# Compression inputs of a sparse-attention trunk: scaled into SBUF in order of parity, moved between partitions by DMA, split once at 128x512

## Chip, core and metric

The kernel runs on one core of one Trainium2 chip. The metric is the time of one execution on the device in microseconds. Engines are named as in the profile: PE is TensorE (PEld its weight loads), DVE VectorE, ACT ScalarE, POOL GpSimd, SP the engine whose queue issues most DMAs.

## What is computed

One layer of a trunk with 256 tokens of width 1024: a sparse attention mixer (16 heads in 4 groups, head width 64), cross attention to 256 memory tokens, and a gated feed-forward layer with a short convolution. The change is in the compression of keys (input 0) and values (input 1) in the mixer. Each input is a 256-wide projection of the normalized tokens, 4 groups of 64. Blocks of 32 tokens at a stride of 16 (15 blocks a group) are flattened to 2048 numbers, a position code is added, and a two-layer network makes one key or value of each:

```python
def _compress(t, pe, w1, w2):
    B, S, G, dk = t.shape
    n_chunks = S // CMP_STRIDE
    r = CMP_BLOCK // CMP_STRIDE
    n_cmp = n_chunks - r + 1
    c = t.reshape(B, n_chunks, CMP_STRIDE, G, dk)
    blk = jnp.concatenate([c[:, j:j + n_cmp] for j in range(r)], axis=2)
    blk = (blk + pe[:, None, :]).transpose(0, 1, 3, 2, 4).reshape(B, n_cmp, G, CMP_BLOCK * dk)
    return jax.nn.gelu(blk @ w1) @ w2
```

## The kernel before

Everything is float32. A matmul operand is split in two parts for TensorE's rounded float32 format: hi, a copy rounded by ACT, and lo, the rest, by DVE (`split_hi`, L191; `split_lo`, L194). `mm3` (L184 to L189) then makes three matmuls of a product: hi x hi, lo x hi, hi x lo. Weights come as chunks of 128 x 2048, in halves of 128 x 1024: SP loads a half into a raw buffer (L112), ACT makes hi (L120), DVE makes lo (L124). Halves are split up to 4 ahead of the matmul that needs them (`half`, L127), and there are 6 buffers of hi and 6 of lo, taken in turn, so the hi of a half waits until the matmuls that read the half six places earlier are through.

The stage around the change is `first` (L667): the projection of input 0 (`compress_in(0)`, PSUM tile pc0), a quarter of the queries (pq0), the projection of input 1 (`compress_in(1)`, pc1), the selected keys (`keys(0)`, pk0), then `hidden(0)` and `hidden(1)`, then `keys(1)` and more queries. `hidden(j)` multiplies the compression's first-layer weights by the prepared input: 16 steps of two matmuls (hi and lo of the weights) into pM0 or pM1, whose stationary operand holds hi and lo of the input side by side. Its result is brought out by ACT (hsb), transposed (pH), and goes through the gelu on DVE and ACT.

The prepared input j is the pair of tiles c2[j][0] and c2[j][1] of 128 partitions x 8 steps x (hi, lo) x 64 columns. Two tokens that follow each other (even and odd, the parity) stand in the two halves of the partitions, and the two groups that a 128-partition projection holds must come side by side in the columns, so data move between the halves of the partitions. Before, `out` in `compress_in` (L459) scales pc in place by the row of reciprocal norms (L462), and then four `split_hi` and four `split_lo` (L475, L478), one for each pair of group half and parity, read 64 partitions of PSUM and write 64 other or equal partitions of SBUF. GpSimd then copies the columns shifted by one block into the second tile (L480) and puts the position code's part pe into the last column (L482). All of `hidden(j)` waits for these copies.

The order on SP and GpSimd is that of the program text (manual schedule). On PE, ACT and DVE a scheduler sets the order when the program is built, by an estimate of when each operation could run. On the chip each engine then works through its list in that order.

The PSUM tag S has two banks, which pc0, pc1, pk0, pM0, pM1 and pk1 take in turn. The scratch tile xT has 8 slices of 256; slice 0 holds the row of reciprocal norms.

## Time and profile before

| | |
|---|---|
| median of 3 runs | 458.88 us (458.44 to 459.89) |
| profiled execution | 459.02 us, span 457.1 us |
| PE busy | 445.2 us (97%) |
| DVE busy | 324.2 us (71%) |
| ACT busy | 288.9 us (63%) |
| POOL busy | 42.7 us (9%) |
| mean granted PE clock | 0.992 |

Times in the trace are us from the span's start; a row's second number is its duration, and a merged row (x4) gives the time of all. The profiled execution is 1.9 us longer than its span, which runs from the first to the last instruction. PE's ends are modelled: matmuls overlap, so the step from one start to the next is what one costs.

### The profile page before, as it was taken

Reading aid. Unit: us, or ns where it says so; the run is one execution under the profiler, and the core shown is the slowest. Engines: PE = TensorE matmul, PEld = TensorE weight load, DVE = VectorE, ACT = ScalarE, POOL = GpSimd, SP = SyncE. Lnnn points to the kernel's source line nnn. Section 1 sums busy time; section 2 is a strip of 40 time slices with the busy share of each in tenths; the row PEclk is TensorE's granted clock in tenths of the full one; section 3 lists DMA queues with packets and bytes.
Section 4 is the critical chain, followed back from the end, with each engine's and each line's share of the span. In section 5 each row is a group of like instructions: output and inputs, shape, how many; then the busy total and the mean of one; then the engine's idle time right before and its main releaser. Section 6 shows DMA issues by size and latency. Waiting matters only on the chain.

```text
span 457.1 us, 8682 instructions
## 1 busy us (share of the span) xinstructions
PE 445.2 (97%) x3276; PEld 412.1 (90%) x3276; DVE 324.2 (71%) x694; ACT 288.9 (63%) x591; POOL 42.7 (9%) x82
## 2 busy tenths in 40 slices
PE   8999799999999999999999999999999999999994
PEld 5999799999998778999998899999999999888984
DVE  4788989798888895846643857878777777745413
ACT  6796689677887886865553757666666666535301
POOL 4332001221200000200000010000000000001003
PEclk9999899999999999999999999999999999999998
DMA  8997775543422005555334437755555555564302
GB/s 293 363 412 261 242 241 167 181 122 111 139 94 92 3 1 181 162 156 187 102 104 170 150 128 210 246 186 184 187 180 185 184 189 179 189 188 151 128 0 93
DMA packets 22077, 77.05 MB, mean 169 GB/s; under 512 B 2579, under 2 KB 3091, under 8 KB 22035
## 3 DMA queue, kind: packets, MB, share of 16 engines
q1 hardware_dynamic: 21312, 74.39, 48.7%
q10 hardware_dynamic: 720, 2.10, 1.4%
q8 instruction: 26, 0.43, 0.4%
q14 instruction: 19, 0.13, 0.1%
HBM read 75.43 MB, written 1.05 MB: 167 GB/s over the span
## 4 chain that ended last, share of the span: by engine, by line
PE 85%; DVE 6%; DMA 4%; ACT 2%; issue 2%; SPq 0%; POOLq 0%; DVEq 0%; ACTq 0%; POOL 0%
PE up L187 8%; PE up L189 8%; PE up L188 8%; PE pd L189 5%; PE pd L187 4%; PE pd L188 4%; PE O L868 2%; DVE lo L124 2%; PE pt L846 2%; DMA raw<-in_w_ks 2%; PE pcq L187 2%; PE pmk L189 2%; PE pmk L188 2%; PE pmk L187 2%; PE pmv L189 2%
## 5 line engine op out<-in xcount | busy, mean ns | idle before, releaser
L124 DVE TENSOR_TENSOR lo<-raw,hi 128x1024 fp32r<-128x1024 f32 x130 | 158.6, 1227 | 60.2 <-ACT hi L120 59.3
L120 ACT ACTIVATE hi<-raw 128x1024 fp32r<-128x1024 f32 x130 | 136.8, 1058 | 55.1 <-PE pd L189 17.7
L187 PE MATMUL up<-h_hi,hi 128*128 128x256 f32 x304 | 86.3, 284 | 0.0
L189 PE MATMUL up<-h_hi,lo 128*128 128x256 f32 x304 | 86.2, 284 | 0.0
L188 PE MATMUL up<-h_lo,hi 128*128 128x256 f32 x304 | 86.2, 284 | 0.0
L188 PEld LDWEIGHTS up<-h_lo,hi 128*128 128x128 f32 x304 | 58.4, 192 | 0.0
L189 PEld LDWEIGHTS up<-h_hi,lo 128*128 128x128 f32 x304 | 58.4, 192 | 0.0
L187 PEld LDWEIGHTS up<-h_hi,hi 128*128 128x128 f32 x304 | 58.4, 192 | 0.0
L189 PE MATMUL pd<-hi,aT_lo 128*128 128x512 f32 (+1 forms) x110 | 38.5, 350 | 0.0
L188 PE MATMUL pd<-lo,aT_hi 128*128 128x512 f32 (+1 forms) x110 | 38.5, 350 | 0.0
L187 PE MATMUL pd<-hi,aT_hi 128*128 128x512 f32 (+1 forms) x110 | 38.4, 349 | 0.0
L832 ACT ACTIVATE pp<-pp,nm 128x128 f32<-128x128 f32 (+1 forms) x64 | 28.4, 447 | 5.8 <-DVE nm L826 5.6
L826 DVE CUSTOM_DVE_ANT_0 pp<-s,tri,nrs 128x128 f32<-128x128 f32 (+1 forms) x64 | 24.1, 412 | 2.4 <-PE pt L846 2.0
L188 PEld LDWEIGHTS pd<-lo,aT_hi 128*128 128x128 f32 x110 | 20.7, 188 | 2.9
L189 PEld LDWEIGHTS pd<-hi,aT_lo 128*128 128x128 f32 x110 | 20.7, 188 | 2.9
L187 PEld LDWEIGHTS pd<-hi,aT_hi 128*128 128x128 f32 x110 | 20.7, 189 | 2.9
L1110 ACT ACTIVATE th<-c 128x256 f32<-128x256 f32 x22 | 9.1, 414 | 22.2 <-DVE c L1108 22.2
L850 ACT ACTIVATE pT<-pt 128x256 f32<-128x256 f32 (+1 forms) x32 | 15.3, 482 | 9.2 <-PE pt L846 8.9
L840 DVE TENSOR_SCALAR pp<-pp,den 128x128 f32<-128x128 f32 (+1 forms) x64 | 19.8, 349 | 0.6
L189 PE MATMUL pmv<-hi,memT_lo 128*128 128x256 f32 x64 | 18.6, 290 | 0.0
L188 PE MATMUL pmv<-lo,memT_hi 128*128 128x256 f32 x64 | 18.5, 289 | 0.0
L189 PE MATMUL pq<-hT_hi,lo 128*128 128x256 f32 x64 | 18.5, 289 | 0.0
(309 smaller groups left out, 1149.2 us busy)
## 6 DMA issues: line engine op xcount, KB each, us to landing
raw<-in_w_up SPq DMA_DIRECT2D x44, 512.0 KB, 4.6
raw<-in_w_dn SPq DMA_DIRECT2D x20, 512.0 KB, 3.8
raw<-in_w_q SPq DMA_DIRECT2D x8, 512.0 KB, 5.1
raw<-in_w_mk SPq DMA_DIRECT2D x8, 512.0 KB, 5.0
raw<-in_w_mv SPq DMA_DIRECT2D x8, 512.0 KB, 3.7
raw<-in_w_out SPq DMA_DIRECT2D x8, 512.0 KB, 3.8
raw<-in_ca_wq SPq DMA_DIRECT2D x8, 512.0 KB, 4.7
raw<-in_ca_wo SPq DMA_DIRECT2D x8, 512.0 KB, 4.2
```

Of the source, the lines that this page charges most:

```text
L120: nc.scalar.activation(his[i][h], raws[i][h], AF.Copy)
L124: nc.vector.tensor_tensor(t, raws[i][h], f(his[i][h]), op=ALU.subtract)
L187: nc.tensor.matmul(ps, lh, rh, start=start, stop=False)
L188: nc.tensor.matmul(ps, lh, rl, start=False, stop=False)
L189: nc.tensor.matmul(ps, ll, rh, start=False, stop=stop)
L826: nc.vector.tensor_tensor_reduce(self.ppv[:, br], sv[:, br], tri[:, 1 - t:], nrs[:, t:t + 1], 3e38, ALU.add, ALU.min, self.nm[:, br:br + 1])
L832: nc.scalar.activation(self.ppv[:, br], self.ppv[:, br], AF.Exp, bias=self.nm[:, br:br + 1], scale=-1.0, accum_out=self.den[:, br:br + 1])
L840: nc.vector.tensor_scalar(self.ppv[:, br], self.ppv[:, br], den[:, br:br + 1], None, op0=ALU.mult)
L846: nc.tensor.transpose(self.pt[:, o:o + P], self.pp[:, o:o + P], ident)
L850: nc.scalar.activation(self.pT[:, :self.w], self.pt[:, :self.w], AF.Copy)
L868: nc.tensor.matmul(O[r:r + DK, m * P:(m + 1) * P], V[:, blk // 2, blk % 2, g, :], group[i].pT[:, blk * P:(blk + 1) * P], start=False, stop ...
L1110: nc.scalar.activation(th, c, AF.Tanh, scale=0.5)
```

## The change

`out` in `compress_in` now scales pc into one slice pair of xT, written in order of parity. Four DMAs on GpSimd's queue, one for each pair of group half and parity, move 64 partitions x 256 numbers each to a second slice pair, where parity stands in the halves of the partitions. After 6 further ticks of the schedule (CW) one `split_hi` and one `split_lo` of 128 x 512 write c2. Columns are now ordered by group first, 16 a group, with the position code's part at the 16th of the first group, so the hidden layer has 64 columns in place of 60 behind its matmuls. The two GpSimd copies by x (hi, lo) become one of 64 x 15 numbers a partition, and the two of pe become one. For input 0 the slices are 6, 7 and 2, 3; for input 1 they are 4, 5 and 6, 7; `keys(0)` and `keys(1)` scale into slices 2, 3 and 4, 5.

```diff
@@ compress_in @@
             NB = 15
-            NC = NB * G
+            NC = 64
+            PEC = NB
...
-                    both = ps.rearrange("p (m s) -> p m s", m=2)
-                    nc.vector.tensor_tensor(both, both, row.unsqueeze(1).to_broadcast([P, 2, S]), op=ALU.mult)
-                    split((B[1][:, :, 0, NC], B[1][:, :, 1, NC], cc[:, o + 8:o + 16]),
-                          (pe[:, 0, :, 0], pe[:, 1, :, 0], cc[:, o:o + 8]))
-                    yield
-                    items = []
+                    v, vp = (xT[:, k:k + 2].rearrange("p k s -> p (k s)") for k in ((6, 2), (4, 6))[j])
+                    v = v.rearrange("p (r m c) -> p r m c", r=2, m=2)
+                    vp = vp.rearrange("p (g c jj) -> p g c jj", g=2, jj=8)
+                    nc.vector.tensor_tensor(v.rearrange("p r m c -> p m c r"),
+                                            ps.rearrange("p (m c r) -> p m c r", m=2, r=2),
+                                            row.rearrange("p (c r) -> p c r", r=2).unsqueeze(1).to_broadcast(
+                                                [P, 2, 128, 2]), op=ALU.mult)
                     for gp in range(2):
                         for par in range(2):
-                            v_ = ps[gp * 64:gp * 64 + 64].rearrange(
-                                "p (m n jj r) -> p m n jj r", m=2, jj=8, r=2)[:, :, :, :, par]
-                            dh, dl = (B[0][par * 64:par * 64 + 64, :, x, :].rearrange(
-                                "p jj (n m gp) -> p m n jj gp", m=2, gp=2)[:, :, :, :, gp] for x in range(2))
-                            items.append((dh, dl, v_))
-                    for hi, lo, v_ in items:
-                        split_hi(hi, v_)
-                    yield
-                    for hi, lo, v_ in items:
-                        split_lo(lo, hi, v_)
-                    for x in range(2):
-                        nc.gpsimd.tensor_copy(B[1][:, :, x, 0:NC], f(B[0][:, :, x, G:16 * G]))
-                    for x in range(2):
-                        nc.gpsimd.tensor_copy(B[0][:, :, x, NC:NC + 1], f(pe[:, x]))
+                            nc.gpsimd.dma_start(vp[par * 64:par * 64 + 64, gp].rearrange("p c jj -> p (c jj)"),
+                                              v[gp * 64:gp * 64 + 64, par].rearrange("p m c -> p (m c)"))
+                    split((B[1][:, :, 0, 0, 0, PEC], B[1][:, :, 1, 0, 0, PEC], cc[:, o + 8:o + 16]),
+                          (pe[:, 0, :, 0], pe[:, 1, :, 0], cc[:, o:o + 8]))
+                    yield from pause(CW)
+                    hi, lo = (B[0][:, :, x].rearrange("p jj g m n -> p g (m n) jj") for x in range(2))
+                    split_hi(hi, vp)
+                    yield
+                    split_lo(lo, hi, vp)
+                    nc.gpsimd.tensor_copy(rows[1][:, :, 0:PEC], f(rows[0][:, :, 1:16]))
+                    nc.gpsimd.tensor_copy(B[0][:, :, :, 0, 0, PEC].rearrange("p jj x -> p x jj"), f(pe[:, :, :, 0]))
                     done.add(f"c2{j}")
```

The rest of the change follows the new order of the columns in `hidden`, `compressed_keys` and `compressed_values`.

The order in which the engines' lists stand moves at two places. In the names c200 and c201 are the two tiles of input 0, c210 and c211 those of input 1, and hi8_1 is the second half of weight chunk 8; chunk 5 is that of pk0, chunks 6 and 7 those of pM0, 8 and 9 those of pM1, 10 that of pk1.

The first place is ACT's list from the projections to the hidden layer. Before:

```order
L120 ACTIVATE hi5_0_363<-raw5_0_361 128x1024
L192 ACTIVATE c200_256<-pc0_260 64x2x16x8 x4
L120 ACTIVATE hi5_1_381<-raw5_1_379 128x1024
L611 ACTIVATE QS_240<-pq0_360 64x512 x2
L120 ACTIVATE hi6_0_456<-raw6_0_454 128x1024
L120 ACTIVATE hi6_1_478<-raw6_1_476 128x1024
L216 ACTIVATE sq_mem0a_1030,ss_mem0a_1029<-mem0_1001 128x512
L192 ACTIVATE c210_449<-pc1_453 64x2x16x8 x4
L894 DMA mem1_1052<-in_mem 128x1024
L120 ACTIVATE hi7_0_523<-raw7_0_521 128x1024
L585 ACTIVATE gsb_583<-pg_559 96x256
L120 ACTIVATE hi7_1_578<-raw7_1_576 128x1024
```

With the change:

```order
L121 ACTIVATE hi7_1_566<-raw7_1_564 128x1024
L193 ACTIVATE w2h_783<-w2k_245 128x256
L121 ACTIVATE hi8_0_627<-raw8_0_625 128x1024
L600 ACTIVATE gt_597<-gt_597,hrs_248 128x48 x2
L121 ACTIVATE hi8_1_644<-raw8_1_642 128x1024
L193 ACTIVATE c200_256<-xT_100 128x64x8
L193 ACTIVATE KH_90<-xT_100 64x2x2x128 x4
L217 ACTIVATE sq_mem1a_1114,ss_mem1a_1113<-mem1_1045 128x512
L193 ACTIVATE c211_446<-cc_71 128x8
L121 ACTIVATE hi9_0_662<-raw9_0_660 128x1024
L121 ACTIVATE hi9_1_676<-raw9_1_674 128x1024
L193 ACTIVATE c210_445<-xT_100 128x64x8
```

and DVE's list over the same stretch, with the change:

```order
L125 TENSOR_TENSOR lo8_0_631<-raw8_0_625,hi8_0_627 128x1024
L603 TENSOR_SCALAR gates_95<-gt_597 128x4x12 x2
L125 TENSOR_TENSOR lo8_1_648<-raw8_1_642,hi8_1_644 128x1024
L197 TENSOR_TENSOR c200_256<-xT_100,c200_256 128x64x8
L498 TENSOR_TENSOR xT_100<-pk0_516,xT_100 128x512
L512 TENSOR_TENSOR KL_91<-xT_100,KH_90 64x2x2x128
L215 SCALAR_TENSOR_TENSOR sq_mem1b_1117,ss_mem1b_1116<-mem1_1045 128x512
L512 TENSOR_TENSOR KL_91<-xT_100,KH_90 64x2x2x128
L197 TENSOR_TENSOR c211_446<-cc_71,c211_446 128x8
L125 TENSOR_TENSOR lo9_0_666<-raw9_0_660,hi9_0_662 128x1024
L125 TENSOR_TENSOR lo9_1_680<-raw9_1_674,hi9_1_676 128x1024
L197 TENSOR_TENSOR c210_445<-xT_100,c210_445 128x64x8
```

The split of input 0 (c200) moved from before the queries' QS to behind hi8_1, that of input 1 (c210) from before hi7_0 to behind hi9_1, and on DVE in the same way.

The second place is GpSimd's list, from the norm's diagonal to the hidden layer's values. Before:

```order
L247 TENSOR_SCALAR dg_x_391<-ident_74,rs_x_101 128x128 x2
L480 CAST c201_257<-c200_256 128x8x60 x2
L482 CAST c200_256<-pe0_258 128x8 x2
L443 TENSOR_SCALAR nrs_247<-rs_x_101 128x2
L444 TENSOR_SCALAR hrs_248<-rs_x_101 128x2
L456 MEMSET c211_450 128x16x3
L480 CAST c211_450<-c210_449 128x8x60 x2
L482 CAST c210_449<-pe1_451 128x8 x2
```

With the change:

```order
L248 TENSOR_SCALAR dg_x_391<-ident_74,rs_x_101 128x128 x2
L475 DMA xT_100<-xT_100 64x256 x4
L444 TENSOR_SCALAR nrs_247<-rs_x_101 128x2
L445 TENSOR_SCALAR hrs_248<-rs_x_101 128x2
L484 CAST c201_257<-c200_256 128x64x15
L485 CAST c200_256<-pe0_258 128x2x8
L461 MEMSET c211_446 128x64
L475 DMA xT_100<-xT_100 64x256 x4
L484 CAST c211_446<-c210_445 128x64x15
L485 CAST c210_445<-pe1_447 128x2x8
```

The DMAs of input 1 stand behind the copies of input 0, and these behind the split of input 0.

## Rows read from the trace of the kernel before

**Rows 1.** Page, busy time, share of the span, instructions.

```profile
PE 445.2 (97%) x3276; PEld 412.1 (90%) x3276; DVE 324.2 (71%) x694; ACT 288.9 (63%) x591; POOL 42.7 (9%) x82
```

**Rows 2.** Busy time by stretch: length, PE, PEld, DVE, ACT, POOL, PEclk, DMA share, GB/s.

```profile
43.10:48.00 4.90, 4.61 (x37) 4.24 (x35) 4.84 (x8) 2.92 (x5) 3.11 (x3) 1.00 0.50 171
48.00:53.50 5.50, 3.12 (x19) 2.29 (x18) 5.44 (x10) 5.38 (x10) 0.00 (x0) 1.00 0.75 254
53.50:57.20 3.70, 3.67 (x18) 3.67 (x19) 3.70 (x6) 2.20 (x4) 0.00 (x0) 0.55 0.72 220
57.20:100.00 42.80, 42.80 (x348) 40.70 (x347) 36.73 (x80) 33.91 (x69) 7.41 (x14) 1.00 0.56 182
100.00:400.00 300.00, 298.75 (x2311) 281.40 (x2311) 222.37 (x526) 194.75 (x430) 11.74 (x20) 1.00 0.46 150
```

**Rows 3.** Waits of PE from 20 to 90 us: total, times, longest.

```profile
PE pM L531 <- DVE lo L124: 1.7, 2, 0.8
PE pM L531 <- ACT hi L120: 0.8, 1, 0.8
PE pgt L589 <- ACT gsb L585: 0.4, 1, 0.4
PE pM L531 <- DVE c L196: 0.3, 1, 0.3
```

**Rows 4.** Timeline of ACT, 26 to 54 us: start, duration, operation.

```profile
27.52 2.59 ACT L192 ACTIVATE c<-pc 64x256 fp32r<-64x256 f32 x4
...
43.75 1.99 ACT L120 ACTIVATE hi<-raw 128x1024 fp32r<-128x1024 f32 x2
...
49.68 0.56 ACT L597 ACTIVATE gt<-gt,hrs 128x48 f32<-128x48 f32 x2
```

**Rows 5.** Timeline of DVE, 29 to 57 us.

```profile
30.14 2.56 DVE L196 TENSOR_TENSOR c<-pc,c 64x256 fp32r<-64x256 f32 x4 [1.27 <-ACT c L192]
...
37.80 0.70 DVE L462 TENSOR_TENSOR pc<-pc,xT 128x512 f32<-128x512 f32 x1
...
47.60 0.25 DVE L594 TENSOR_TENSOR gt<-pgt,gt 128x96 f32<-128x96 f32 x1
47.76 2.35 DVE L124 TENSOR_TENSOR lo<-raw,hi 128x1024 fp32r<-128x1024 f32 x2
...
51.45 0.28 DVE L600 TENSOR_SCALAR gates<-gt 128x48 f32<-128x48 f32 x2
```

**Rows 6.** Timeline of POOL, 29 to 48 us.

```profile
30.17 0.59 POOL L480 CAST c<-c 128x480 fp32r<-128x480 f32 x1 [5.74 <-ACT c L192]
32.76 1.65 POOL L480 CAST c<-c 128x480 fp32r<-128x480 f32 x1 [2.00 <-DVE c L196]
34.35 0.33 POOL L482 CAST c<-pe 128x8 fp32r<-128x8 f32 x2
...
45.33 1.52 POOL L482 CAST c<-pe 128x8 fp32r<-128x8 f32 x2
```

**Rows 7.** Timeline of PE, 42 to 57 us.

```profile
42.65 0.38 PE L589 MATMUL pgt<-ident,gsb 96*128 96x96 f32 x2 [0.39 <-ACT gsb L585]
...
43.25 0.28 PE L189 MATMUL pk<-hT_hi,lo 128*128 128x256 f32 x1
43.82 0.36 PE L531 MATMUL pM<-hi,c 128*128 128x256 f32 x1 [0.29 <-DVE c L196]
...
47.55 0.28 PE L531 MATMUL pM<-lo,c 128*128 128x256 f32 x1
...
56.84 0.42 PE L531 MATMUL pM<-lo,c 128*128 128x256 f32 x1
57.05 0.40 PE L189 MATMUL pk<-hT_hi,lo 128*128 128x256 f32 x1
```

**Rows 8.** DMA issues on SP, in the timeline and by transfer (KB, us to landing).

```profile
27.76 0.33 SPq L675 DMA_DIRECT2D w2k<-in_w_ck  x1
...
out<-y SPq DMA_DIRECT2D x1, 256.0 KB, 2.0
...
w2k<-in_w_ck SPq DMA_DIRECT2D x1, 128.0 KB, 9.4
```

More of the change, by code (lines that the diff above doesn't have):

```diff
@@ L88, in trunk_kernel @@
     HW = 4
+    CW = 6
     PAC = 18
@@ L448, in trunk_kernel @@
             NB = 15
-            NC = NB * G
+            NC = 64
+            PEC = NB
             c2 = []
             def compress_in(j):
-                B = [cp.tile([P, 8, 2, 64], F32R, name=f"c2{j}{i}") for i in range(2)]
+                B = [cp.tile([P, 8, 2, 2, 2, 16], F32R, name=f"c2{j}{i}") for i in range(2)]
+                rows = [z.rearrange("p jj x g m n -> p (jj x g m) n") for z in B]
                 pe = cp.tile([P, 2, 8, 1], F32R, name=f"pe{j}")
                 o = C_PE + j * 16
-                nc.gpsimd.memset(f(B[1][:, :, :, NC + 1:64]), 0.0)
+                nc.gpsimd.memset(f(rows[1][:, :, PEC]), 0.0)
                 c2.append(B)
@@ L528, in hidden @@
                     half, jj = divmod(kt, 8)
-                    st = c2[j][half][:, jj].rearrange("p x c -> p (x c)")
+                    st = c2[j][half][:, jj].rearrange("p x g m n -> p (x g m n)")
                     for x, w in enumerate(wtile(c0 + half, jj, 0, HID)):
@@ L544, in out @@
                     yield
-                    hl = cp.tile([P, 2, NC + 1], F32, tag="hl", name=f"hl{j}")
-                    nc.vector.tensor_copy(hl, pH[:, :, 1, 0:NC + 1])
-                    nc.vector.tensor_tensor(hl, pH[:, :, 0, 0:NC + 1], hl, op=ALU.add)
+                    hl = cp.tile([P, 2, NC], F32, tag="hl", name=f"hl{j}")
+                    nc.vector.tensor_copy(hl, pH[:, :, 1])
+                    nc.vector.tensor_tensor(hl, pH[:, :, 0], hl, op=ALU.add)
                     u = cp.tile([P, 2, NC], F32, tag="u", name=f"u{j}")
-                    nc.vector.tensor_tensor(u, hl[:, :, 0:NC], hl[:, :, NC:NC + 1].to_broadcast([P, 2, NC]),
+                    nc.vector.tensor_tensor(u, hl, hl[:, :, PEC:PEC + 1].to_broadcast([P, 2, NC]),
                                             op=ALU.add)
@@ L638, in compressed_keys @@
                 yield
-                kcv = pkc[:, :NC].rearrange("p (n g) -> p g n", g=G)
+                kcv = pkc[:, :NC].rearrange("p (gp m n) -> p m gp n", gp=2, m=2)[:, :, :, 0:NB]
                 for g in range(G):
                     c = slice((g % 2) * 32, (g % 2) * 32 + NB)
-                    nc.scalar.activation(KHc[:, g, c], kcv[:, g], AF.Copy)
+                    nc.scalar.activation(KHc[:, g, c], kcv[:, g // 2, g % 2], AF.Copy)
                 yield
@@ L646, in compressed_keys @@
                     c = slice((g % 2) * 32, (g % 2) * 32 + NB)
-                    nc.vector.tensor_tensor(KLc[own, g, c], kcv[own, g], f(KHc[own, g, c]), op=ALU.subtract)
+                    nc.vector.tensor_tensor(KLc[own, g, c], kcv[own, g // 2, g % 2], f(KHc[own, g, c]), op=ALU.subtract)
             def compressed_values():
                 gv = cp.tile([P, 2, G, 16], F32, name="gv")
-                nc.gpsimd.tensor_scalar(gv[:, :, :, 0:NB].rearrange("p a g n -> p a n g"),
-                                        gel[:, 1].rearrange("p a (n g) -> p a n g", g=G),
-                                        0.5, None, op0=ALU.mult)
+                for gp in range(2):
+                    nc.gpsimd.tensor_scalar(gv[:, :, gp::2, 0:NB],
+                                            gel[:, 1].rearrange("p a (gp m n) -> p a gp m n", gp=2, m=2)[:, :, gp, :, 0:NB],
+                                            0.5, None, op0=ALU.mult)
                 yield from pause(HW)
```

## Prediction

> **What bounds the kernel now.** TensorE is busy for 445.2 of 457.1 us [rows 1], so only its idle time and its clock can be won or lost. The busy time by stretch shows where those lie [rows 2]: from 57.2 to 100 us it never idles, from 100 to 400 us for 1.25 us, but from 48.0 to 53.5 us it works only 3.12 of 5.50 us, and for the 3.70 us behind that the granted clock is 0.55, mostly the lower of its two levels, 1.2 and 2.4 GHz. This is the stage of pM0 and pM1, the 2 x 32 matmuls of the compression's hidden layer, and the table of waits names what they wait for there [rows 3]: weight splits on DVE (1.7 us) and ACT (0.8 us), once DVE's read of the PSUM bank that pM0 takes over (0.3 us), and before that pgt for gsb (0.4 us). Inputs of the compression are never late for pM0 now: its splits stand at 27.5 us on ACT [rows 4] and 30.1 us on DVE [rows 5], its GpSimd copies end at about 34.7 us [rows 6], and pM0 starts at 43.82 us [rows 7]. The profiled execution took 459.02 us, 0.14 above the median of 458.88, so its sum stands for the median.
>
> **What goes.** Per input, four ACT and four DVE operations of 64x256 (2.59 and 2.56 us [rows 4, 5]) become one of each at 128x512. TensorE's matmuls keep their number and, up to pM0, their order. With the second four gone from ACT (38.5 to 41.1 us), gsb is ready in time and the 0.39 us wait goes: the last matmul of pk0 starts at 42.86 instead of 43.25, and pk0 ends at 43.1. The PSUM bank comes free with the scaling, so the 0.3 us go too. In the order, however, both splits now stand much later, and I follow the first.
>
> **First split.** pgt, at 42.26 without its wait, takes 0.38 us [rows 7], then the two gt operations on DVE some 0.25 each [rows 5]: 43.1. Two tanh on ACT, 0.56 [rows 4]: 43.7. Then hi8_1, half of the 1.99 us of two [rows 4]: 44.7; it could not come much earlier, since it takes hi5_1's buffer, which the last but one matmul of pk0 reads. Only behind it does ACT split the first input. The price of a 128x512 split into places 512 bytes apart is on no row; it lies between 0.70, a 512-wide DVE operation with an orderly output [rows 5], and 1.30, two of the present 0.65, should the scattered output cost as much per element. I take 1.0, the middle: 45.7. On DVE lo8_0 and the two gates operations (0.28) are done by 44.6, lo8_1 takes half of 2.35 [rows 5] from 44.7 to 45.9, and the low part 1.0 more (0.70 to 1.30): 47.0. GpSimd then copies 960 elements a partition; 480 took 0.59 with no weight split beside it [rows 6], so 1.2: 48.2. The copy of pe (0.33 for two of 8 [rows 6], now one of 16) takes 0.3: 48.5, and **pM0 starts at 48.6**, 4.8 us late. With both ends of each price it is 48.1 to 51 (the latter if both copies wait for DVE, as below). So TensorE idles 5.5 us where it now idles 0.7.
>
> **pM0.** Now it runs from 43.82 to about 47.7, one matmul each 0.118 us [rows 7]. After the stretch with 2.4 us of idle the clock was low for 3.7 us, in which 18 matmuls went through, 0.206 each [rows 2]; after 5.5 us of idle I take the same: 18 in 3.7 us, 14 in 1.7 us, 5.4 in all, so to 54.0. If the clock stays up it is 3.8, to 52.4.
>
> **Second split.** Its four transfers stand on GpSimd's queue behind the first copies, so they cannot be issued before 48.5. No row shows a transfer of that queue. Bounds: below, four issues of 0.33 and the shortest landing in the trace, 2.0 us for 256 KB, 3.3 together; above, the same issues and 9.4 us, the 128 KB of w2k [rows 8], 10.7. I take 4.6, near the lower end, because w2k landed while the DMA engines were full and they are at 0.50 from 43.1 to 48 us [rows 2]: 53.1. On ACT hi9_0 and hi9_1 wait for pM0's first 8 and 16 matmuls (16 are through at 51.9): hi9_1 ends at 53.0. So both roads meet: high part to 54.1, low part on DVE, behind lo9_1, to 55.2. The copy then meets lo10_0, which stands next on DVE. Beside a lo a 480-wide copy took 1.65 instead of 0.59, and the two of pe 1.52 instead of 0.33 [rows 6]. If this were a slower rate, 960 elements would take 3.3; as a wait of fixed length they take 1.2 + 1.06 = 2.3. I take the wait, since the copy at 32.76 ends about half a microsecond after that lo. The Trainium skill, "SBUF — State Buffer", section "Who interferes with whom", states the same as a lock: of a DVE operation with two SBUF inputs and a GpSimd operation reading SBUF, the later one blocks entirely. By the rate the sum below would be 1.0 larger. So the copy ends at 57.5, that of pe at 59.0 (0.3 + 1.2), and **pM1 starts at 59.0** (without the meeting 56.8): 5 us of idle again.
>
> **The sum.** pM1 takes 5.4 us, once more with the low clock, pH0 0.2 before it: 64.6. Now all of pM1 is through at 57.05 [rows 7], with two matmuls of pk1 among it, 0.4 us; without them 56.6. The waits for lo and hi that lie in this time now (2.5 us [rows 3]) and the present low clock are inside that difference: the waits vanish, since 6 halves of weights are split by then. The loss is 64.6 - 56.6 = 8.0 us. Behind it TensorE has no idle time in which to catch up [rows 2]. What else moves costs nothing: the first four transfers leave when the scaling is done, at about 27.5 us, where the first split begins now [rows 4], and have until 44.7; the scaling writes to SBUF in place of PSUM under 16 us of TensorE work; the later order in the attention changes on ACT, DVE and PE, where 1.25 us are idle now, so within 1 us either way. 459.02 + 8.0 = **467.0 us**.
>
> **Rivals.**
> - *A lighter loss.* Each price at its low end, no low clock: pM0 48.1 to 51.9, hi9_0 and hi9_1 at 51.1, transfers at 51.3, high part to 52.0, low part to 53.0, copies to 54.4, pM1 from 54.5 to 58.5 with pH0: +1.9, so 460.9; with the low clock in pM0 alone about 462.6. For it: ACT and DVE are less loaded than now. Chance 0.18.
> - *The transfers decide.* If each of the four is waited out before the next is started, or they land as late as w2k, the second split starts at 57 to 59 instead of 53.1, and all behind it is 4 to 6 us later: 471 to 473. The Trainium skill, "DMA: Bandwidth & Descriptors", section "Anatomy of one DMA — SWDGE (gpsimd) path", gives some 2.0 us plus size by 436 GB/s for one such transfer; an estimate from that is 2.15 us each, 8.6 in a row, and a time of 471; in parallel it speaks for the forecast. No run here has shown either yet. Chance 0.17.
> - *Idle only gathered: no change.* If the second input is ready when pM0 ends and the clock stays up, pM0 and pM1 run from 48.6 without a break, 7.6 + 0.2 us, to 56.4, against 56.6 now: 458.8. Against it: the transfers stand behind the first copies on GpSimd, and they, two splits and two copies cannot all pass in 3.8 us: the low ends above leave 6.4 between the starts of pM0 and pM1. Chance 0.07.
> - *Faster.* If the first split went through in the gaps of ACT and DVE before pk0 ends, pM0 would start at 43.1 with its weights ahead: all waits of [rows 3], 3.2 us, and the low clock, 18 x (0.206 - 0.118) = 1.6 us, would go: 454.2. The point that decides is whether ACT reaches the first split before pk0's matmuls release hi5_1's buffer, at about 42.9. The order puts it behind hi8_1, which needs that buffer. Chance 0.04.
>
> **How the numbers follow.** The forecast has 0.54. The range of 461.0 to 472.0 takes in the lighter loss and most of the case of the transfers. About 0.3%, 1.4 us, is what a measurement of this kernel can tell from no change: faster 0.04, same 0.07, slower 0.89.
>
> **What would show it.** Right: idle TensorE of 4 to 6 us between pk0 and pM0, ended by a GpSimd copy; a second of 3 to 6 us before pM1, also ended by GpSimd; the granted clock near 0.55 in part of both; no wait of pM for lo or hi; transfers of some 3 to 5 us from issue to landing. Wrong: pM0 starting before 46 us, GpSimd's copies over before TensorE asks for them, or a stretch behind 70 us that idles by more than now.

## The result, and the profile after

| | before | with the change |
|---|---|---|
| median of the runs measured together | 459.03 us (458.44 to 459.89, 4 runs) | 465.90 us (464.96 to 467.27, 4 runs) |
| profiled execution | 459.02 us, span 457.1 us | 464.96 us, span 463.2 us |

The ratio is 1.0147, with a 95% interval of 1.0125 to 1.0168: slower by 6.9 us. The profiled execution is the fastest of its four; against that of before it lost 5.94 us. The line of busy times, to be held against [rows 1]:

```profile
PE 445.1 (96%) x3276; PEld 413.3 (89%) x3276; DVE 322.8 (70%) x688; ACT 285.9 (62%) x585; POOL 46.0 (10%) x87
```

TensorE is busy for as long as before, so what was lost is idle time. The busy time by stretch of the changed kernel (columns as in [rows 2]: length, PE, PEld, DVE, ACT, POOL, PEclk, DMA share, GB/s) shows where:

```profile
42.90:48.30 5.40, 0.19 (x2) 0.00 (x0) 4.44 (x7) 3.06 (x5) 1.19 (x3) 0.98 0.93 343
48.30:51.60 3.30, 3.25 (x15) 3.25 (x16) 2.16 (x5) 3.21 (x8) 2.13 (x5) 0.51 0.63 191
53.70:58.60 4.90, 0.49 (x3) 0.20 (x2) 4.90 (x5) 2.44 (x4) 2.99 (x2) 0.98 0.70 214
58.60:61.80 3.20, 3.16 (x15) 3.16 (x16) 1.64 (x7) 1.77 (x4) 0.00 (x0) 0.50 0.44 164
100.00:400.00 300.00, 299.55 (x2345) 283.61 (x2344) 223.95 (x535) 196.48 (x436) 12.49 (x22) 1.00 0.45 150
```

Twice TensorE stands still, for 5.3 and 4.4 us, and twice the clock behind it is low for some 3.2 us, in which 15 matmuls pass; before, it was low once, for 3.7 us [rows 2]. The waits of TensorE from 20 to 90 us, against [rows 3], name GpSimd's copies in place of the weight splits:

```profile
PE pM L534 <- POOL c L485: 7.3, 2, 5.3
PE pH L545 <- ACT hsb L541: 2.4, 1, 2.4
```

GpSimd's copy of the position code's part (L485) ends both stops. Within the second TensorE also waits 2.4 us for hsb, which costs nothing by itself, since pM1 could not start before that copy. The three matmuls of its timeline that end a wait, against [rows 7] (start, duration):

```profile
48.35 0.58 PE L534 MATMUL pM<-hi,c 128*128 128x256 f32 x1 [5.27 <-POOL c L485]
56.19 0.44 PE L545 MATMUL pH<-ident,hsb 128*128 128x128 f32 x2 [2.44 <-ACT hsb L541]
58.64 0.58 PE L534 MATMUL pM<-hi,c 128*128 128x256 f32 x1 [2.01 <-POOL c L485]
```

The road to those copies is read from three more timelines. ACT, against [rows 4]: the two high parts are `c<-xT`, both without idle time in front, so ACT came to them late; their data were there.

```profile
43.74 1.04 ACT L121 ACTIVATE hi<-raw 128x1024 fp32r<-128x1024 f32 x1
44.68 1.08 ACT L193 ACTIVATE c<-xT 128x512 fp32r<-128x512 f32 x1
47.73 2.58 ACT L193 ACTIVATE KH<-xT 64x512 fp32r<-64x512 f32 x4 [1.96 <-DVE xT L498]
...
51.06 2.00 ACT L121 ACTIVATE hi<-raw 128x1024 fp32r<-128x1024 f32 x2
52.96 1.11 ACT L193 ACTIVATE c<-xT 128x512 fp32r<-128x512 f32 x1
```

DVE, against [rows 5]: each low part follows, the scaling of pk0 (L498), for which ACT's KH waits, stands behind the first, and behind the second stand the two lo of chunk 10, which take 3.14 us where the two of chunk 9 took 2.36.

```profile
45.95 1.02 DVE L197 TENSOR_TENSOR c<-xT,c 128x512 fp32r<-128x512 f32 x1
47.01 0.69 DVE L498 TENSOR_TENSOR xT<-pk,xT 128x512 f32<-128x512 f32 x1
...
52.13 2.36 DVE L125 TENSOR_TENSOR lo<-raw,hi 128x1024 fp32r<-128x1024 f32 x2 [0.76 <-ACT hi L121]
54.41 1.06 DVE L197 TENSOR_TENSOR c<-xT,c 128x512 fp32r<-128x512 f32 x1
55.38 3.14 DVE L125 TENSOR_TENSOR lo<-raw,hi 128x1024 fp32r<-128x1024 f32 x2
```

POOL, against [rows 6]: the same two copies take 0.98 and 0.21 us alone, and 1.91 and 1.08 beside those lo.

```profile
47.04 0.98 POOL L484 CAST c<-c 128x960 fp32r<-128x960 f32 x1 [16.46 <-DVE c L197]
48.09 0.21 POOL L485 CAST c<-pe 128x16 fp32r<-128x16 f32 x1
...
48.32 2.11 POOL L475 DMA_DIRECT2D xT<-xT  x4
55.53 1.91 POOL L484 CAST c<-c 128x960 fp32r<-128x960 f32 x1 [5.10 <-DVE c L197]
57.50 1.08 POOL L485 CAST c<-pe 128x16 fp32r<-128x16 f32 x1
```

Last, the transfers, by tile in the stretch from 47 to 56 us; [rows 8] had no row of this queue:

```profile
L475 POOL DMA_DIRECT2D xT<-xT x4: 518/522/567, 48.3 to 49.9; - x4
DMA to landing us min/median/max: 1.9/2.2/2.7
```

The last of the second four was issued at 49.9 us and had landed by 52.6 at the latest, ahead of the split at 52.96.

### The profile page after: what moved, and what is told of

Its sections match the earlier page's. It is cut to its first block, busy times and chain, and to the rows that moved or that the text cites. A ratio compares the mean times of both kernels' runs of the same rounds, so it can differ in the third digit from the quotient of the medians.

```text
span 463.2 us, 8681 instructions
## 1 busy us (share of the span) xinstructions
PE 445.1 (96%) x3276; PEld 413.3 (89%) x3276; DVE 322.8 (70%) x688; ACT 285.9 (62%) x585; POOL 46.0 (10%) x87
## 4 chain that ended last, share of the span: by engine, by line
PE 92%; DVE 3%; ACT 1%; issue 1%; DMA 1%; POOL 1%; POOLq 0%; DVEq 0%; ACTq 0%
PE up L190 8%; PE up L188 8%; PE up L189 8%; PE pd L190 4%; PE pd L188 4%; PE pd L189 4%; PE pv L403 3%; PE O L872 2%; PE pt L850 2%; PE pq L188 2%; PE pq L189 2%; PE pmk L190 2%; PE pq L190 2%; PE pcq L188 2%; PE pcq L189 2%; PE pmv L189 2%
## 5 line engine op out<-in xcount | busy, mean ns | idle before, releaser
L1148 POOL TENSOR_TENSOR xw<-x_sb,wfin 128x512 f32<-128x512 f32 (+1 forms) x2 | 3.9, 1953 | 156.1 <-DVE x_sb L1131 156.1
L844 DVE TENSOR_SCALAR pp<-pp,den 128x128 f32<-128x128 f32 (+1 forms) x64 | 18.5, 329 | 0.7
L190 PE MATMUL pmk<-memT_hi,lo 128*128 128x256 f32 x64 | 18.9, 295 | 0.0
```

What stands on the lines that cost most here:

```text
L190: nc.tensor.matmul(ps, ll, rh, start=False, stop=stop)
L844: nc.vector.tensor_scalar(self.ppv[:, br], self.ppv[:, br], den[:, br:br + 1], None, op0=ALU.mult)
```

## The experiments

My theory: the time is lost because both splits stand late in the lists of ACT and DVE; what follows from it is idle time, the low clock behind it and the meeting of copy and lo. Rivals: the transfers themselves are late, the clock alone makes the loss, or GpSimd's copies do. In most runs the lists are held to a chosen order, by a chain of dependencies without waits that follows a table of places (run 1 shows how; later diffs show only the rows that move). The names in these diffs leave out the chunk: hi_0_519 is hi7_0, hi_1_644 hi8_1, lo_1_648 lo8_1, lo_0_666 and lo_1_680 are the two of chunk 9, lo_0_695 and lo_1_711 those of chunk 10; c_256 is c200, c_445 or c_443 is c210.

The table serves all runs: from each profiled execution the start of pk0's last matmul, the starts of the first and last matmul of pM0 and of pM1, and two differences. "From pk0" is the span less the first column, which takes out that the stage begins at 42.7 to 44.5 us in different executions. "Behind pM1" is the span less the last start of pM1. Each ratio is to executions of the kernel before that were measured along with the run, with a 95% interval.

| kernel | pk0 last | pM0 | pM1 | from pk0 | behind pM1 | median of runs, ratio to before |
|---|---|---|---|---|---|---|
| before | 43.25 | 43.82 to 47.55 | 47.83 to 56.84 | 413.85 | 400.26 | |
| the change | 42.81 | 48.35 to 53.48 | 58.64 to 63.82 | 420.39 | 399.38 | 465.90, 1.0147 [1.0125, 1.0168] |
| 1 first split early | 44.51 | 44.67 to 48.43 | 59.74 to 65.05 | 419.89 | 399.35 | 465.77, 1.0153 [1.0106, 1.0199] |
| 2 transfers early | 42.91 | 48.45 to 54.31 | 58.74 to 64.04 | 420.59 | 399.46 | 465.93, 1.0156 [1.0101, 1.0211] |
| 3 idle time filled | 43.50 | 49.12 to 52.77 | 60.49 to 64.17 | 420.10 | 399.43 | 465.03, 1.0136 [1.0092, 1.0181] |
| 4 no transfers | 43.08 | 43.19 to 46.71 | 46.83 to 52.38 | 409.32 | 400.02 | 454.52, 0.9902 [0.9869, 0.9935] |
| 5 copies alone | 42.69 | 48.23 to 54.07 | 56.71 to 60.50 | 417.81 | 400.00 | 462.63, 1.0074 [1.0053, 1.0096] |
| 6 both splits early | 44.29 | 44.52 to 48.13 | 52.28 to 57.59 | 418.81 | 405.51 | 464.12, 1.0100 [1.0082, 1.0118] |
| 7 values first | 43.41 | 43.85 to 47.58 | 48.03 to 52.15 | 422.29 | 413.55 | 467.12, 1.0172 [1.0156, 1.0188] |
| 8 SyncE's queue | 43.60 | 43.72 to 51.90 | 52.11 to 57.22 | 417.40 | 403.78 | 462.37, 1.0068 [1.0046, 1.0091] |
| 9 as 6, later lists held | 43.76 | 43.88 to 47.40 | 50.64 to 56.40 | 412.94 | 400.30 | 458.38, 0.9983 [0.9964, 1.0001] |
| 10 as 7, later lists held | 42.77 | 43.03 to 46.65 | 47.08 to 51.28 | 411.03 | 402.52 | 457.27, 0.9952 [0.9931, 0.9973] |
| 11 before, values first | 43.00 | 43.12 to 46.77 | 46.88 to 54.18 | 411.60 | 400.42 | 457.30, 0.9969 [0.9953, 0.9985] |

**Run 1, the first split early.** Both lists are those of the change but for one row on each engine; DVE's moves in the same way:

```diff
@@ ACT's list @@
 L898 DMA mem_1045<-in_mem 128x1024
+L193 ACTIVATE c_256<-xT 128x64x8
 L121 ACTIVATE hi_0_519<-raw_0_517 128x1024
...
 L121 ACTIVATE hi_1_644<-raw_1_642 128x1024
-L193 ACTIVATE c_256<-xT 128x64x8
 L193 ACTIVATE KH<-xT 64x2x2x128 x4
@@ how a list is held @@
+    for engine, ranks in HOLD.items():
+        own = [i for i in block if i.engine == getattr(mybir.EngineType, engine) and i.name not in skip]
+        for a, b in zip(ranks, ranks[1:]):
+            tc.add_manual_dep(own[b], own[a].name,
+                              mybir.DependencyInfo(mybir.DependencyClass.NoSync, mybir.DependencyReason.DATA),
+                              reason="order")
```

> Only the split of input 0 moves: on ScalarE from behind hi8_1 to in front of hi7_0, on VectorE from behind lo8_1 to in front of lo7_0; the lists of ScalarE, VectorE and TensorE are held otherwise as in the changed kernel, GpSimd's and SyncE's too. Mine, that the second split's start is set by ScalarE's list behind pk0 and not by the first split: pM0 starts at 43.1 to 43.6 instead of 48.35, but KH still waits for pk0's scaling, so the second split on ScalarE begins 0 to 1.1 us earlier than 52.96, pM1 starts at 57.5 to 58.6 and ends at 62.8 to 63.9; time 463.8 to 465. Rival, that each late split costs its own idle time and the transfers of input 1, which now leave 8 us earlier, let pM1 follow: pM1 ends near 58.6, time about 459.6.

The first stop of TensorE is gone: pM0 starts 0.16 us after pk0's last matmul, at the full clock. And yet only 0.5 us are won from pk0 on (419.89 for 420.39). ACT's list again shows the second split without idle time in front:

```profile
52.16 1.99 ACT L121 ACTIVATE hi<-raw 128x1024 fp32r<-128x1024 f32 x2
54.06 1.09 ACT L193 ACTIVATE c<-xT 128x512 fp32r<-128x512 f32 x1
```

So the second split hangs on ACT's own list, not on pM0, and the 5 us are merely spent ahead of pM1, as the waits of TensorE from 20 to 90 us show:

```profile
PE pH L545 <- ACT hsb L541: 8.5, 1, 8.5
PE pM L534 <- POOL c L485: 1.8, 1, 1.8
```

The two stops are not two separate losses. The median of 465.77 lies 0.8 above the expected range and 6.2 above the rival's time; in the profiled execution the whole stage began 1.7 us later than in the change's, which is why the comparison goes from pk0.

**Run 2, the transfers early.** Input 1's four transfers stand ahead of input 0's copies on GpSimd's queue:

```diff
+                    for work in todo:
+                        work()
+                    todo.clear()
...
-                    nc.gpsimd.tensor_copy(rows[1][:, :, 0:PEC], f(rows[0][:, :, 1:16]))
-                    nc.gpsimd.tensor_copy(B[0][:, :, :, 0, 0, PEC].rearrange("p jj x -> p x jj"), f(pe[:, :, :, 0]))
+                    if j == 0:
+                        todo.append(copies)
+                    else:
+                        copies()
```

> The four transfers of input 1 stand in front of the copies of input 0 on GpSimd's queue, so they leave at about 36.4 us instead of 48.3; the lists of all other engines are held as in the changed kernel. Mine: ScalarE had no idle time in front of the second split, so nothing moves: pM0 at 48.3, pM1 at 58.4 to 58.7, time 465.0 within 0.7. Rival, the transfers decide the second split: it begins at 51 or earlier, pM1 1.5 to 2 us earlier, time about 463.

They are issued 11.5 us sooner, and nothing moves (420.59 for 420.39); the median of 465.93 lies 0.2 above the expected range. POOL's and ACT's timelines:

```profile
36.79 2.11 POOL L476 DMA_DIRECT2D xT<-xT  x4 [4.92 <-DVE xT L470]
```

```profile
53.05 1.16 ACT L193 ACTIVATE c<-xT 128x512 fp32r<-128x512 f32 x1
```

The transfers' lateness is not what the stage waits for. A side reading: issued here, where the DMA engines' share is 1.04 from 36 to 44 us, the four took 7.5 us in the median to land, for 2.2 when issued at 48.3 to 49.9 us:

```profile
xT<-xT POOLq DMA_DIRECT2D x4, 64.0 KB, 7.5
```

**Run 3, the idle time filled.** TensorE works through matmuls whose result is overwritten (44 ahead of pM0, 31 and 19 around pH0), all else in the order of the change:

```diff
+                for k in range(FILL[j]):
+                    h = hT[0][:, k % KT]
+                    filler.append(nc.tensor.matmul(pM[0:M, 0:HID], h[:, 0:M], h, start=True, stop=True).ins)
```

> TensorE multiplies without use while it would be idle: 44 matmuls of 128x256 into pM0's bank before pM0, 31 into pM1's bank behind pM0 and 19 behind pH0; the real matmuls then overwrite the bank. All other lists are held as in the changed kernel. Mine, that the low clock follows the idle time, and that pM1's start hangs on ScalarE's list: granted clock 1.00 in pM0 and pM1, each takes 3.8 us instead of 5.2 to 5.3, pM0 starts at 48.3 and pM1 at 58.4 to 58.7 as before the edit, pM1 ends at 62.3 instead of 63.94; time 463.4, so 1.5 us less and not 3. Rival, that the low clock comes from something else than idle time: 5.2 us each, time 465. Second rival, that pM0's end decides what follows: 3 us less, 462.

```profile
42.90:49.00 6.10, 6.10 (x52) 5.95 (x51) 4.76 (x8) 3.31 (x6) 1.13 (x3) 1.00 0.85 306
49.00:53.00 4.00, 3.93 (x34) 3.88 (x34) 2.25 (x6) 3.92 (x9) 2.21 (x6) 1.00 0.50 147
53.00:60.40 7.40, 6.21 (x53) 6.01 (x52) 6.78 (x7) 4.04 (x5) 3.00 (x2) 1.00 0.54 179
60.40:64.30 3.90, 3.90 (x36) 3.90 (x35) 2.42 (x7) 2.77 (x6) 0.00 (x0) 1.00 0.16 64
```

The granted clock stays at 1.00, and the first and last start of pM0 lie 3.65 us apart, those of pM1 3.68, for 5.13 and 5.18: the low clock costs 1.5 us in each. But only 0.3 us came out of it, from pk0 on. pM0's gain does not reach pM1, as in run 1, and most of pM1's is lost again, because the second split comes 1.0 us later, counted from pk0: here it waits for a transfer, whose four took up to 3.9 us to land, for up to 2.7 with the change.

```profile
54.68 1.15 ACT L195 ACTIVATE c<-xT 128x512 fp32r<-128x512 f32 x1 [0.86 <-DMA xT<-xT]
```

The measured gain is a miss of the expectation; what the clock is worth, it shows. Whether the fillers delayed the transfer stays open, and two executions cannot tell a gain of 0.3 us from one of 1.5 by their times.

**Run 4, no transfers.** The transfers are left out and the splits read the scaled buffer, so half of the values stand in the wrong partitions; the work of the engines is the same. The scheduler makes its own lists.

```diff
-                    for gp in range(2):
-                        for par in range(2):
-                            nc.gpsimd.dma_start(vp[par * 64:par * 64 + 64, gp].rearrange("p c jj -> p (c jj)"),
-                                              v[gp * 64:gp * 64 + 64, par].rearrange("p m c -> p (m c)"))
+                    vp = v.rearrange("p r m c -> p (r m c)").rearrange("p (g c jj) -> p g c jj", g=2, jj=8)
```

> The eight transfers are left out: the splits read the scaled buffer itself, so the values of the two halves stand in the wrong partitions; the lists are the scheduler's own. Mine, that only its estimate of the transfers puts the splits late: it sets both splits in front of hi7_0, pM0 starts at 43.1 and pM1 within 0.5 us of pM0's end, at 46.9 to 47.4, with at most 1.5 us of waiting for weights behind it and the clock at 1.00; pM1 ends at 50.8 to 52.3, time 453.5 to 455.5. Rival, that the full-width splits and the copies themselves (the lock with VectorE, ScalarE's load) keep the stage late: pM1 ends at 56 or later, time 459 or more.

Both splits move to the front of the lists, as ACT's timeline shows, and pM1 starts 0.12 us after pM0's last matmul:

```profile
27.98 1.18 ACT L193 ACTIVATE c<-xT 128x512 fp32r<-128x512 f32 x1 [0.37 <-DVE xT L469]
...
36.70 1.14 ACT L193 ACTIVATE c<-xT 128x512 fp32r<-128x512 f32 x1 [2.23 <-DVE xT L469]
```

454.5 us is what the change is worth if moving the data cost nothing: 1% faster than before. With the transfers it is 11.4 us more. How much of this is the transfers' own time and how much the place that the scheduler gives to the splits when there are transfers, run 9 tells.

**Run 5, the copies alone.** The two lo of chunk 10 stand behind pH0's first steps on DVE, so that nothing runs there beside the second copies:

```diff
@@ DVE's list @@
 L197 TENSOR_TENSOR c_445<-xT,c_445 128x64x8
-L125 TENSOR_TENSOR lo_0_695<-raw_0_689,hi_0_691 128x1024
-L125 TENSOR_TENSOR lo_1_711<-raw_1_705,hi_1_707 128x1024
 L549 COPY hl_736<-pH_729 128x128
 L550 TENSOR_TENSOR hl_736<-pH_729,hl_736 128x128
 L552 TENSOR_TENSOR u_739<-hl_736 128x128
+L125 TENSOR_TENSOR lo_0_695<-raw_0_689,hi_0_691 128x1024
+L125 TENSOR_TENSOR lo_1_711<-raw_1_705,hi_1_707 128x1024
```

> VectorE's splits lo10_0 and lo10_1 move from in front of hl0 to behind u0, so that no split of weights stands beside GpSimd's copies of input 1; the lists of ScalarE, VectorE and TensorE are otherwise held as in the changed kernel. Mine, that copy and split exclude each other: the copy of 960 elements takes 0.98 us in place of 1.91 and that of pe 0.21 in place of 1.08, pM1 starts 1.8 us earlier, at 56.7 to 57.0 when pk0 ends as in the changed kernel, and ends 1.8 us earlier; time 463.2. Rival, that the copy is slow for its own sake (columns 16 apart): 1.9 and 1.1 us again, time 465.

As expected. POOL's timeline, and the stretch of pM1:

```profile
55.40 0.98 POOL L484 CAST c<-c 128x960 fp32r<-128x960 f32 x1 [5.09 <-DVE c L197]
56.45 0.21 POOL L485 CAST c<-pe 128x16 fp32r<-128x16 f32 x1
```

```profile
56.70:60.70 4.00, 3.99 (x33) 3.99 (x34) 3.52 (x8) 0.73 (x3) 0.00 (x0) 1.00 0.51 182
```

The meeting cost (1.91 + 1.08) - (0.98 + 0.21) = 1.8 us, and the shorter idle time ahead of pM1 (2.6 us between pM0's last start and pM1's first, for 5.2) leaves the clock up, worth 1.4 more. Of these 3.2 us 2.6 arrive at the end.

**Run 6, both splits early.** Both splits early, input 1's transfers as in run 2, the second split behind hi9_0 on ACT and its low part behind lo8_1 on DVE, so that KH and KL now come behind it; ACT and DVE are held in this stage, what comes later is left to the scheduler.

```diff
@@ DVE's list @@
 L125 TENSOR_TENSOR lo_1_648<-raw_1_642,hi_1_644 128x1024
...
+L197 TENSOR_TENSOR c_443<-xT,c_443 128x64x8
+L507 TENSOR_TENSOR xT<-pk_514,xT 128x512
 L125 TENSOR_TENSOR lo_0_666<-raw_0_660,hi_0_662 128x1024
 L125 TENSOR_TENSOR lo_1_680<-raw_1_674,hi_1_676 128x1024
-L197 TENSOR_TENSOR c_445<-xT,c_445 128x64x8
```

> Both splits moved to where their transfers can have landed, within the order of the program: input 0 behind sq_mem0a (ScalarE) and sq_mem0b (VectorE), input 1 behind hi9_0 and lo8_1, the transfers of input 1 in front of the copies of input 0 on GpSimd, and KH and KL of the selected keys behind hi9_1 and lo10_1. Mine: pM0 follows pk0 without idle time, at 43.1; the transfers of input 1 land at 44 to 46.5, so its split runs at 46 to 48.5, the copies end at 49.7 to 51, and pM1 starts at 50 to 51 after 3 to 4 us of idle time and ends at 54 to 56.5; time 456 to 459, about that of the kernel before. Rival, that ScalarE's and VectorE's relief of 3 us each is all that counts: as without transfers, 454.5. Second rival, that the stage stays as late as with one split moved: 464.

A miss. The stage is 7.7 us shorter (from pk0's last start to pM1's last 13.3 us, for 21.0), but 6.1 us of it are lost behind pM1 (405.51 for 399.38). The waits of TensorE from 20 to 110 us, and a stretch behind 80 us:

```profile
PE pM L543 <- POOL c L490: 3.9, 1, 3.9
PE pst L750 <- DVE QS L629: 3.6, 1, 3.6
```

```profile
80.00:85.00 5.00, 3.26 (x11) 2.49 (x12) 3.85 (x5) 4.91 (x10) 3.17 (x6) 0.51 0.32 107
```

TensorE comes to the scores (pst) before DVE has the queries, and pays the low clock once more.

**Run 7, the values first.** The projection of input 1 ahead of the queries, so that they cover its split; its transfers go to the free tile pcT; the copies of pe lie on DVE; the stage held as in run 6.

```diff
-                yield from queries(0)
                 yield from compress_in(1)
+                yield from queries(0)
...
+                    if j:
+                        vp = pcT[:, 0:2].rearrange("p a t q -> p (a t q)")
...
-                    nc.gpsimd.tensor_copy(B[0][:, :, :, 0, 0, PEC].rearrange("p jj x -> p x jj"), f(pe[:, :, :, 0]))
+                        nc.vector.tensor_copy(B[0][:, :, :, 0, 0, PEC].rearrange("p jj x -> p x jj"), f(pe[:, :, :, 0]))
```

> As the one before, and the projection of input 1 is made ahead of the queries' first quarter (weight chunks in that order too), so that its transfers leave some 4 us earlier; they land in a piece of pcT, which is not yet in use. Input 1 is split behind hi8_0 and lo8_0, the copies of pe are VectorE's, and no split of weights stands beside GpSimd's copy of input 1. Mine: transfers of input 1 leave at 32 to 35 and land by 42, pM0 starts at 43.1, pM1 at 46.8 to 47.6 with the clock at 1.00 throughout, and ends at 50.7 to 52.5; time 453.5 to 456, faster than both kernels. Rival, that the transfers or the weights are late in this order too: pM1 ends at 56 or later, 459 or more.

The same miss, larger: the stage is repaired (pM0 and pM1 from 43.85 to 52.15), and 14 us are lost behind it, of which the longest single wait is

```profile
PE pq L188 <- DVE QS L631: 3.4, 1, 3.4
```

**Run 8, SyncE's queue.** The eight transfers are issued by SyncE; nothing is held.

```diff
-                            nc.gpsimd.dma_start(vp[par * 64:par * 64 + 64, gp].rearrange("p c jj -> p (c jj)"),
+                            nc.sync.dma_start(vp[par * 64:par * 64 + 64, gp].rearrange("p c jj -> p (c jj)"),
```

> The eight transfers are issued on SyncE's queue in place of GpSimd's, one word; lists of ScalarE, VectorE and TensorE are the scheduler's own, and it sets the splits in front of hi6_0 and behind hi7_0. Mine: the splits are no longer behind weights, but SyncE waits for both scalings (27.5 and 36.2 us), and the loads of chunks 6 to 9 behind them leave 6 to 10 us later; pM0 starts at 43 to 45, pM1 waits for weights; time 456 to 462. Rival, that the estimate alone decides: as without transfers, 454.5. Second rival, that the held loads starve TensorE: over 466.

```profile
PE pM L534 <- ACT hi L121: 2.5, 1, 2.5
PE pst L741 <- DVE QS L620: 2.3, 1, 2.3
PE pM L534 <- DVE lo L125: 0.9, 1, 0.9
```

No copy is late any more; the transfers now stand in the queue of the weights' loads (the four of w_cv leave from 43.34 us on, with the change from 30.14), pM0 waits for weight splits, and the scores for the queries. The waits fell into pM0 and not, as expected, into pM1, and the median lies 0.4 above the expected range. This doesn't tell the theories apart well: the queue and the lists changed together.

**Runs 9 and 10, the later lists held too.** As runs 6 and 7 (in 9, too, the copies of pe lie on DVE), but ACT, DVE and TensorE are held well beyond the stage, to the order that the scheduler makes when it is shown no transfers, and only the splits are put where the transfers have landed. DVE's list in run 9, in part:

```diff
+L197 TENSOR_TENSOR c_443<-xT,c_443 128x64x8
+L507 TENSOR_TENSOR xT<-pk_514,xT 128x512
+L490 CAST c_443<-pe_445 128x2x8
 L125 TENSOR_TENSOR lo_0_666<-raw_0_660,hi_0_662 128x1024
 L125 TENSOR_TENSOR lo_1_680<-raw_1_674,hi_1_676 128x1024
-L197 TENSOR_TENSOR c_445<-xT,c_445 128x64x8
 L125 TENSOR_TENSOR lo_0_695<-raw_0_689,hi_0_691 128x1024
```

> Transfers stay on GpSimd's queue, and the projections keep the change's order, but ScalarE, VectorE and TensorE are held, far beyond this stage too, to the order that the scheduler makes when it is shown no transfers; input 1's transfers are issued ahead of input 0's copies, the pe copies lie on VectorE, and the splits stand where the transfers have landed. My theory: the 6.9 us are lost because the splits stand late in the engines' lists, and the 5 us that the sixth run lost behind the stage came from later lists that the scheduler made by its own estimate of the transfers. Then pM1 starts near 50 and ends at 54 to 55.5, and the part behind it takes 399.5 to 400.5 us: 455.5 to 458.5. Rival: the later waits (TensorE for VectorE's states, 3 to 4 us, low clock between 80 and 100 us) come whenever the stage ends early, whatever the order: 462 or more.

> The same, and the projection of the values of input 1 is put ahead of that of the queries, which covers the splits of input 1. My theory: pM1 starts at 46.8 to 48 and ends near 52 at the full clock, and nothing is lost behind it: 452.5 to 456, faster than the kernel before. Rival: the later waits that the seventh run showed (TensorE for VectorE's states, 3.4 us, low clock between 70 and 80 us) belong to this order of projections and not to the scheduler's estimate: 461 or more.

Run 9's waits of TensorE from 20 to 110 us are down to one in the stage, and the later ones are gone:

```profile
PE pM L543 <- DVE c L490: 3.0, 1, 3.0
```

Behind pM1 it takes 400.30 us, as before the change, for 405.51 in run 6. So the later loss belonged to the lists, and not to a stage that ends early. The time lies inside the expectation, though pM1 ends at 56.5, 1.0 later than expected. With the order of its projections left alone, the change thus comes to the time of before: 0.9983 [0.9964, 1.0001]. Of the 11.4 us between run 4 and the change, 7.5 come back by the order of the lists and the place of the copies of pe; the other 3.9 stay with the transfers. The four of input 1, issued from 37.66 us on at a DMA share of 1.04, take 7.2 us in the median to land (6.6 to 7.7), and now ACT does wait for the last of them; in run 4 the same split starts at 36.70:

```profile
47.03 1.10 ACT L193 ACTIVATE c<-xT 128x512 fp32r<-128x512 f32 x1 [0.40 <-DMA xT<-xT]
```

So pM1 waits those 3.0 us for its input, and the granted clock is 0.83 from 50 to 60 us. That all of the 3.9 is this landing is argued: run 4's lists and its copies of pe differ from run 9's too.

Run 10 has no such wait, and its longest is the one for hsb:

```profile
PE pH L556 <- ACT hsb L552: 1.1, 1, 1.1
PE pq L188 <- ACT hi L121: 0.5, 1, 0.5
PE pM L545 <- DVE c L492: 0.2, 1, 0.2
```

By its median it is 8.6 us faster than the change, and it is faster than before by 0.48%, 0.27 to 0.69%; its profiled execution took 455.59 us, inside the expectation, its median of 457.27 lies 1.3 above it. Behind pM1 it still loses 2.2 us against run 9.

**Run 11, the order of the projections alone.** Run 10 differs from before in two things, the new split and the values ahead of the queries. So the second is given to the kernel before:

```diff
-                yield from queries(0)
                 yield from compress_in(1)
+                yield from queries(0)
```

> The kernel before, with one edit: the projection of the values of input 1 (and its weights' loads) stands ahead of the quarter of the queries, as in the tenth run; the lists are the scheduler's own. My theory: the gain of the tenth run comes from the new split at 128x512 once it stands in time, since the four plus four splits of the kernel before take ACT and DVE 3.2 us and block halves of weights; the order of projections alone gives the kernel before nothing: 458 to 460.5, within 0.3% of it. Rival: the order of projections is what made the tenth run faster, and the kernel before gains by it as well: 457 or less.

It falls on the rival's side: 0.9969 [0.9953, 0.9985], though at 457.3 just above the rival's bound. The kernel before gains as well, with nothing held; of the four waits in [rows 3] those for gsb and for c are gone, and that for lo is shorter:

```profile
PE pM L531 <- DVE lo L124: 1.0, 2, 0.8
PE pM L531 <- ACT hi L120: 0.8, 1, 0.8
```

So by the medians two thirds of what run 10 shows against before come with the order of the projections. What the new split adds, between 0.9952 and 0.9969, is within the intervals and stays open.

## Why the prediction held, step by step

| step of the prediction | forecast | measured |
|---|---|---|
| last matmul of pk0 starts | 42.86 | 42.81 |
| hi8_1 ends | 44.7 | 44.78 |
| high part, low part of a 128x512 split | 1.0, 1.0 | 1.08, 1.02 |
| first copies | 1.2 and 0.3, to 48.5 | 0.98 and 0.21, to 48.30 |
| pM0 | 48.6 to 54.0 | 48.35 to 53.6 |
| transfers landed | 53.1 | by 52.6 |
| hi9_1 ends | 53.0 | 53.06 |
| second split, high and low end | 54.1, 55.2 | 54.07, 55.47 |
| second copies, beside lo10 | 2.3 and 1.5, to 59.0 | 1.91 and 1.08, to 58.58 |
| pM1 | 59.0 to 64.6 | 58.64 to 63.94 |
| loss at the end of pM1 | 8.0 | 7.3 |
| behind it | 0, within 1 either way | gain of about 1.2 |

(Ends of pM0 and pM1 are the last start and one step, 0.12 us.) **The forecast's mechanism is the one that came**, at each of its places but one (hi9_1, below), and the range held the time. Its marks came as written: two stops of 5.3 and 4.4 us (the latter the two waits around pH0) ended by GpSimd's copy, the granted clock near 0.5 behind both, no wait of pM for lo or hi. The mark of 3 to 5 us for the transfers holds for the four together, 4.3 us from the first issue to the last landing; a single one took 1.9 to 2.7.

**What was too large.** The sum ran 2.0 us above the profiled execution, 1.1 above the median. 0.66 us of it arose by the end of pM1: the second copies took 0.7 less than the 3.8 forecast and pM1 with pH0 0.3 less than 5.6, while the low part ended 0.3 later. For the meeting with lo10 I had taken fixed waits of 1.06 and 1.2 us, and it added 0.93 and 0.87; alone the copy cost less than the doubled 480-wide row said. The Trainium skill, "SBUF — State Buffer", section "Who interferes with whom", describes an exclusive lock. The rows fit one, in both directions: the copy started at 55.53, 0.15 us after the first lo, and became 0.93 us longer; the pair of lo takes 2.36 us undisturbed at 52.13 us and 3.14 around the copy, 0.78 longer; the copy of pe starts at 57.50 and ends at 58.58, just behind the second lo (58.52). Taken singly, the first lo keeps its 1.22 us while the copy stands, and the second takes 2.00. By a slower rate for GpSimd alone the second lo would not have grown, and by one for both the first would have grown too.

About 1.2 us more lie behind pM1 (399.26 us from its end, for 457.1 - 56.6 = 400.5). In the stretch from 100 to 400 us the idle time fell from 1.25 [rows 2] to 0.45. "Behind it TensorE has no idle time in which to catch up" was therefore wrong by that 0.8; the clause that the new order there could give up to 1 us either way covered it. The other 0.4 is not located, and which row of the lists brought it was not tried.

**Where reason and result differ.** The prediction hung the second stop on the first: hi9_0 and hi9_1 were to wait for pM0's first 8 and 16 matmuls, through at 51.9, and so to end at 53.0. They ended at 53.06, but pM0 did not hold them. ACT came to them at 51.06 without idle time, behind KH, which had waited 1.96 us for DVE's scaling of pk0; and in run 1, where the 16th matmul of pM0 starts at 46.55, the pair still starts at 52.16. KH and that scaling are in no term of the sum. So this step was right by luck, and with it the start of the second split: pM0's start and its clock, which the prediction worked out with care, hardly bear on the end. Run 1 shows that the first stop is worth 0.5 us by itself, and in run 3 pM0 is 1.5 us shorter and pM1 starts no sooner. What sets the end is ACT's list up to the second split (KH, hi9_0, hi9_1), the split, the meeting of copy and lo, pM1; from the second split on the forecast's reasons are those of the trace.

**The rivals.** *A lighter loss* needed the copies at their low ends and the clock up: run 5 makes that true for the second copies and pM1, and gives 462.6, the 462.6 that this rival named for the low clock in pM0 alone. *The transfers decide* falls for the lists of the change: the four were issued 0.52 us apart and landed within 1.9 to 2.7 us each, in parallel, and run 2 sends them 11.5 us sooner for nothing. The estimate of 2.15 us for one such transfer by the Trainium skill, "DMA: Bandwidth & Descriptors", section "Anatomy of one DMA — SWDGE (gpsimd) path", agrees with the median of 2.2 here; at a DMA share of 1.03 to 1.04 the same 64 KB took 6.4 us in the median (the change's first four) to 7.5 (run 2), so there the measurement decides. *No change* asked for a second input that is ready when pM0 ends, *faster* for a first split ahead of pk0's end. The lists gave neither. Run 4 gives both, without the moving, and comes out at 454.5 where *faster* said 454.2; run 9 comes out at 458.4 where *no change* said 458.8, but by another road, with pM0 at 43.88 and a wait of 3.0 us ahead of pM1.

**Shown and argued.** Shown: that the place of the splits and not the moment of the transfers' issue sets the loss in the lists of the change (runs 6 and 9 against 2), that 3.9 us remain with the transfers once the splits stand early (9 against 4), that the meeting with lo10 is 1.8 us of it and the clock behind it 1.4 (run 5), and that the later loss of runs 6 and 7 lies in the later lists (9 and 10). Argued only: that the scheduler puts the splits late because it holds the transfers to be slow; run 4 shows that they move to the front without transfers, but the estimate itself is in no trace.

## What to carry to other kernels

A transfer put between two operations can cost more by the place that an automatic order gives to its reader than by its own time: look at the reader in its engine's list, and at whether there is idle time before it, before blaming the DMA. When a stall is repaired by hand, the lists behind it were made for the slow stage, and hand the gain back; hold or rebuild them too. And when the repaired version beats the old kernel, give the old kernel the same reordering before crediting the change.

## What the runs showed that I had not expected

- The same 64 KB transfer within SBUF took 1.9 to 2.7 us to land at a DMA share of 0.63 (48.3 to 51.6 us) and 7.5 in the median at one of 1.04.
- The meeting of GpSimd's copy and DVE's lo costs DVE nearly as much (0.78 us) as GpSimd (0.93).
- A stop of 5 us costs another 1.5 us through the clock; matmuls without use in the idle time kept the granted clock at 1.00 (run 3), and in run 5, behind a stop of 2.6 us, it was 1.00 too; in the kernel before, behind 2.4 us of idle time in pieces, it was 0.55 [rows 2].
- Taking out the whole stop of 5 us ahead of pM0 gave 0.5 us; the swap of two projections, in the kernel before, gave 1.5 (medians of 458.80 and 457.30).
